# A gather, a running sum and a matmul: TensorE's program rolled into a loop, GpSimd's drain in its own stream, and another start

## The chip, the cores and the metric

The kernel runs on one core of one Trainium2 chip. Times are device microseconds of one execution. The five engines that matter here are TensorE (PE, with its weight loads shown apart as PEld), VectorE (DVE), ScalarE (ACT), GpSimd (POOL) and SyncE (SP), which only issues transfers. They run side by side and meet at counters (semaphores): an instruction raises a counter when it is done, and another waits until the counter has reached a value.

## What is computed

There are 16 batches. In each, 2048 rows of 512 numbers are picked out of 4096 by sorted indices, summed cumulatively along the 2048, and multiplied by one 512 x 512 matrix:

```python
B, S, N, D = (16, 4096, 2048, 512)
gathered = x[b_idx, indices, :].copy()
cs = np.cumsum(gathered, axis=1)
return np.matmul(cs, w).astype(np.float32)
```

So 67 MB are read by rows of 2 KB, and 67 MB are written.

## The kernel before

A *tile* is 128 gathered rows (T = 256 of them), a *group* is two tiles (G = 128). Every group passes through the same stations, and each engine has its own stream, written out in full, one instruction after the other.

- `gather(t)` on POOL (L108): one indirect transfer brings the 128 rows of tile t into `g32`. There is room for NG = 16 tiles; from the 17th on POOL waits until the tile's room is free, that is, until the cast of eight groups earlier is done (`s_c`).
- `cast(g)` on ACT (L120): both tiles of a group become 16-bit in `g16` (NH = 3 buffers), when both transfers have landed.
- `sums(t)` on PE (L128): four small matmuls with a triangular matrix `ut` put the running sums of a tile, turned on its side, into PSUM `pa` (NA = 4 buffers).
- `carry(t)` on DVE (L143, L148): adds the last column of the tile before and writes `cst` in 16 bits. This is the chain that goes through a whole batch.
- `project(g, j)` on PE (L160): four matmuls with the weights `w16` give half of a group's output in PSUM `pb` (NB = 2 buffers).
- `drain(g)` on ACT (L172): copies the group's output into `ob` (NO = 8 buffers).
- `store(g)` on SP (L178): writes it out.

The order within each engine is fixed by the program. PE's runs two groups ahead with the sums: sums of the first four tiles, then for each group g: the first sum of group g+2, the first product of g, the second sum, the second product. ACT's alternates: the cast of group g+3, then the drain of group g. So the cast of group g+4 stands behind the drain of group g, and the sums of group g+4 behind that cast.

In the beginning SP loads the indices of two tiles in a form that POOL can use directly (`idx_first`), then all indices (`idx64`), then the weights in one transfer of 1 MB. The rest of the indices is made usable on the way: DVE turns them into floats (L225), PE transposes them (L229), DVE turns them back (L234). POOL makes the constants. ACT casts group 0, then all of the weights (L252), then the next groups.

At the end SP waits for the last eight stores. The block is left by `tile_critical(no_gpsimd_drain=False)` (L78), which lets GpSimd drain after that.

Of the kernel before, what the change touches and what calls it, by code (L numbers as in the profile page):

```python
# [27 lines left out]
def kernel(  # L28
# [19 lines left out]
    FIRST = R  # L48
    NG = 16
    NH = 3  # L50
# [3 lines left out]
    NO = 8  # L54
    AH = 2
# [14 lines left out]
    ident = const.tile([P, P], FP32)  # L70
    g32 = [const.tile([P, R, D], FP32, name=f"g32_{i}") for i in range(NG // R)]
# [6 lines left out]
    ctx.enter_context(tc.tile_critical(no_gpsimd_drain=False))  # L78

    def sem(name):  # L80
        return tc.alloc_semaphore(name)

    s_first, s_w, s_ut, s_wc, s_if, s_pt, s_prep = (
        sem(f"s_{n}") for n in ("first", "w", "ut", "wc", "if", "pt", "prep")
    )
    s_idx = [sem(f"s_idx{k}") for k in range(KI)]
    s_g = [sem(f"s_g{i}") for i in range(NG)]
# [11 lines left out]
    def gather(t):  # L99
        g, r = divmod(t, R)  # L100
        pool.need(s_c, g + 1 - NG // R)
        if t < FIRST:
            pool.need(s_first, 16)
            ap = idx_first[:, t, 0:1]
        else:
            pool.need(s_prep, t // P + 1)
            ap = idxg[:, t // P, t % P : t % P + 1]
        nc.gpsimd.indirect_dma_start(  # L108
            out=g32[g % (NG // R)][:, r, :],
            out_offset=None,  # L110
            in_=x_flat,
            in_offset=bass.IndirectOffsetOnAxis(ap=ap, axis=0),
            element_offset=(t // NT) * S * D,
        ).then_inc(s_g[t % NG], 16)
# [7 lines left out]
    def sums(t):  # L122
        g, r = divmod(t, R)
        pe.need(s_c, g + 1)
        pe.need(s_ut, 4)
        pe.need(s_d, t - NA + 1)
        for c in range(DC):
            mm = nc.tensor.matmul(  # L128
                out=pa[t % NA][:, c],
                lhsT=g16[g % NH][:, r, c * P : (c + 1) * P],  # L130
                rhs=ut[:],
                start=(c == 0),
                stop=(c == DC - 1),
            )
        mm.then_inc(s_a, 1)
# [19 lines left out]
    def project(g, j):  # L155
        pe.need(s_wc, 1)
        pe.need(s_d, R * (g + 1))
        pe.need(s_e, g - NB + 1)
# [20 lines left out]


    with nc.allow_non_contiguous_dma(reason="a few indices, one per partition"):
        nc.sync.dma_start(
            out=idx_first[:],
            in_=indices[0, 0 : FIRST * P].bitcast(U32).rearrange("(t p w) -> p t w", p=P, w=2),
        ).then_inc(s_first, 16)
# [5 lines left out]
    nc.sync.dma_start(out=w32[:], in_=w.rearrange("(c p) d -> p c d", p=P)).then_inc(s_w, 16)  # L191
    for g in range(G):
        store(g)
    for g in range(G - NO, G):
        sp.need(s_o[g % NO], 16 * (g // NO + 1))

# [22 lines left out]
    for t in range(T):  # L219
        gather(t)  # L220


    for k in range(KI):
        dve.need(s_idx[k], 16)
        nc.vector.tensor_copy(out=idxf[:, k, :], in_=idx64[:, k, 0::2]).then_inc(s_if, 1)  # L225
    for k in range(KI):
# [4 lines left out]
        ).then_inc(s_pt, 1)  # L231
    for k in range(KI):
        dve.need(s_pt, k + 1)
        nc.vector.tensor_copy(out=idxg[:, k, :], in_=pb[k % NB][:, 0, :P]).then_inc(s_prep, 1)  # L234
    for t in range(T):
        carry(t)


    for t in range(R * AH):
        sums(t)  # L240
    pe.need(s_prep, KI)
    for g in range(G):
        for j in range(R):
            t = R * (g + AH) + j
            if t < T:
                sums(t)
            project(g, j)


    cast(0)  # L250
    act.need(s_w, 16)
    nc.scalar.copy(out=w16[:], in_=w32[:]).then_inc(s_wc, 1)  # L252
    for g in range(1, AH + 1):
        cast(g)
    for g in range(G):
        if g + AH + 1 < G:
            cast(g + AH + 1)
        drain(g)

# [29 lines left out]
```

## Time and profile before

| | us |
|---|---|
| four runs | 424.21, 434.3, 428.37, 464.36; median 431.34 |
| the profiled execution | 424.21 |
| its span | 422.5 |
| PE busy | 313.4 (74%) |
| PEld busy | 156.0 (37%) |
| ACT busy | 253.0 (60%) |
| POOL busy | 243.8 (58%) |
| DVE busy | 177.9 (42%) |
| moved | 135.92 MB, mean 322 GB/s |

The span is the time between the first and the last instruction of the profiled execution. A busy share is a mean over the whole span. The page also cuts the span into 40 slices of 10.56 us and gives for each the busy share of an engine in tenths (9 is 90% or more), the share of full clock that TensorE was granted, the mean busy share of the 16 DMA engines and the rate. A timeline gives the start, the length, the engine, the line, the operation with its operands, a count, and in brackets the idle time before it and what ended it; "remote" and "issue" stand where the profile shows no instruction that did. The ends of matmuls in it are modelled.

### The profile page before, as it was taken

What the parts mean: (1) busy time and instruction counts of PE and PEld (TensorE: products, weight loads), DVE (VectorE), ACT (ScalarE), POOL (GpSimd) and SP (SyncE); (2) the same over time, 40 slices, a digit from 0 to 9 for tenths busy, and PEclk for the clock granted to TensorE, in tenths of its full rate; (3) what the DMA queues carried; (4) which work ended last, traced back from release to release, by engine and by line L of the source; (5) the groups of instructions that cost most, each with busy time, mean ns of one, the idle gap of its engine ahead of it and who ended that gap; (6) DMA issues with size and microseconds to landing.
All of it is one profiled execution on the core that took longest, in us unless ns stands there. A gap on an engine that the chain in (4) does not pass through costs nothing.

```text
span 422.5 us, 5833 instructions
## 1 busy us (share of the span) xinstructions
PE 313.4 (74%) x2050; PEld 156.0 (37%) x2050; DVE 177.9 (42%) x260; ACT 253.0 (60%) x258; POOL 243.8 (58%) x264
## 2 busy tenths in 40 slices
PE   0723979775968688778787787878778787877990
PEld 0411534332534344334333343433334343333540
DVE  0302443443443445344444444444444444444640
ACT  1512655664755557566666766666676666667870
POOL 6773666555656475666666666666666666666000
PEclk9976789899899698999999999999999999999997
DMA  7775899899899899999999999999999999999752
GB/s 231 210 211 201 284 339 340 321 332 342 296 364 330 296 331 317 341 369 359 356 356 349 363 354 355 358 358 355 354 359 349 358 353 358 357 360 351 302 239 110
DMA packets 40029, 135.92 MB, mean 322 GB/s; under 512 B 6465, under 2 KB 6721, under 8 KB 40001
## 3 DMA queue, kind: packets, MB, share of 16 engines
q0 software_dynamic: 20480, 67.13, 49.1%
q1 hardware_dynamic: 19520, 68.43, 41.4%
q8 instruction: 17, 0.28, 0.3%
q14 instruction: 12, 0.09, 0.1%
HBM read 68.42 MB, written 67.11 MB: 321 GB/s over the span
## 4 chain that ended last, share of the span: by engine, by line
PE 71%; issue 16%; another core or an unknown queue 5%; ACT 3%; POOL 2%; DMA 1%; ACTq 0%; SPq 0%
PE pb L160 53%; PE pa L128 17%; ACT g L120 3%; POOL g L108 2%; DMA g<-in_x_dram,idxg 1%; DMA idx_first<-in_indices_dram 0%; ACT ob L172 0%; ACTq L23 0%; SPq L284 0%; SPq L78 0%
## 5 line engine op out<-in xcount | busy, mean ns | idle before, releaser
L108 POOL DMA_INDIRECT g<-in_x_dram,idxg x254 | 240.6, 947 | 144.3 <-issue 111.9
L160 PE MATMUL pb<-w,cst 128*128 128x512 f16 x1024 | 275.3, 394 | 0.0
L148 DVE TENSOR_TENSOR cst<-pa,cst 128x512 f16<-128x512 f32 x240 | 166.0, 692 | 209.3 <-PE pa L128 106.1
L172 ACT COPY ob<-pb 128x1024 f32<-128x1024 f32 x128 | 129.6, 1013 | 150.7 <-PE pb L160 104.3
L128 PE MATMUL pa<-ut,g 128*128 128x128 f16 x1024 | 104.8, 228 | 94.5 <-issue 62.1
L128 PEld LDWEIGHTS pa<-ut,g 128*128 128x128 f16 x1024 | 73.1, 102 | 184.8 <-issue 112.2
L120 ACT CAST g<-g 128x1024 f16<-128x1024 f32 x128 | 134.0, 1048 | 0.6 <-issue 0.6
L160 PEld LDWEIGHTS pb<-w,cst 128*128 128x128 f16 x1024 | 93.2, 101 | 66.6 <-issue 9.2
L143 DVE CAST cst<-pa 128x512 f16<-128x512 f32 x16 | 11.0, 690 | 17.1 <-PE pa L128 17.1
L120 ACT ACT_TABLE_LOAD x1 | 1.3, 1283 | 9.3 <-DMA g<-in_x_dram,idx_first 9.3
L229 PE MATMUL pb<-ident,idxf 128*128 128x128 f32 x2 | 0.7, 457 | 4.5 <-DVE idxf L225 4.5
L108 POOL DMA_INDIRECT g<-in_x_dram,idx_first x2 | 2.1, 1044 | 1.5 <-DMA idx_first<-in_indices_dram 1.2
L225 DVE CAST idxf<-idx 128x128 f32<-128x128 uint32 x2 | 0.5, 227 | 4.2 <-DMA idx<-in_indices_dram 4.1
L229 PEld LDWEIGHTS pb<-ident,idxf 128*128 128x128 f32 x2 | 0.4, 182 | 4.5 <-issue 4.5
L252 ACT CAST w<-w 128x2048 f16<-128x2048 f32 x1 | 1.9, 1893 | 0.0
L234 DVE CAST idxg<-pb 128x128 uint32<-128x128 f32 x2 | 0.6, 292 | 0.3 <-PE pb L229 0.3
L198 POOL MEMSET ident<- 128x128 f32 x1 | 0.2, 205 | 0.5 <-SPq L78 0.5
L201 POOL TENSOR_SCALAR_AFFINE_SELECT ident<-ident 128x128 f32<-128x128 f32 x1 | 0.3, 288 | 0.1
L210 POOL TENSOR_SCALAR_AFFINE_SELECT ut<-ut 128x128 f16<-128x128 f16 x1 | 0.3, 291 | 0.0
L273 POOL MEMSET const-float32-0.0<- 128x1 f32 x1 | 0.1, 100 | 0.3 <-issue 0.3
L199 POOL MEMSET ut<- 128x128 f16 x1 | 0.2, 205 | 0.0
L273 POOL MEMSET const-uint8-127<- 128x1 uint8 x1 | 0.1, 117 | 0.0
(2 smaller groups left out, 0.2 us busy)
## 6 DMA issues: line engine op xcount, KB each, us to landing
out_dram<-ob SPq DMA_DIRECT2D x128, 512.0 KB
g<-in_x_dram,idxg POOLq DMA_INDIRECT x254
w<-in_w_dram SPq DMA_DIRECT2D x1, 1024.0 KB, 5.4
idx<-in_indices_dram SPq DMA_DIRECT2D x2, 128.0 KB, 2.5
g<-in_x_dram,idx_first POOLq DMA_INDIRECT x2
idx_first<-in_indices_dram SPq DMA_DIRECT2D x1, 2.0 KB, 1.9
```

The source lines that it names most:

```text
L108: nc.gpsimd.indirect_dma_start(out=g32[g % (NG // R)][:, r, :], out_offset=None, in_=x_flat, in_offset=bass.IndirectOffsetOnAxis(ap=ap, ax ...
L120: nc.scalar.copy(out=g16[g % NH][:], in_=g32[g % (NG // R)][:]).then_inc(s_c, 1)
L128: mm = nc.tensor.matmul(out=pa[t % NA][:, c], lhsT=g16[g % NH][:, r, c * P : (c + 1) * P], rhs=ut[:], start=(c == 0), stop=(c == DC - 1),)
L143: nc.vector.tensor_copy(out=dst, in_=pa[t % NA][:]).then_inc(s_d, 1)
L148: nc.vector.tensor_tensor(out=dst, in0=pa[t % NA][:], in1=last.unsqueeze(2).broadcast_to([P, DC, R, Q]), op=mybir.AluOpType.add,).then_inc ...
L160: mm = nc.tensor.matmul(out=pb[g % NB][:, j], lhsT=cst[g % NC][:, c, j, :], rhs=w16[:, c, :], start=(c == 0), stop=(c == DC - 1),)
L172: nc.scalar.copy(out=ob[g % NO][:], in_=pb[g % NB][:]).then_inc(s_e, 1)
L201: nc.gpsimd.affine_select(out=ident[:], in_=ident[:], compare_op=mybir.AluOpType.is_equal, fill=0.0, base=0, pattern=[[-1, P]], channel_mu ...
L225: nc.vector.tensor_copy(out=idxf[:, k, :], in_=idx64[:, k, 0::2]).then_inc(s_if, 1)
L229: nc.tensor.transpose(out=pb[k % NB][:, 0, :P], in_=idxf[:, k, :], identity=ident[:]).then_inc(s_pt, 1)
L234: nc.vector.tensor_copy(out=idxg[:, k, :], in_=pb[k % NB][:, 0, :P]).then_inc(s_prep, 1)
L252: nc.scalar.copy(out=w16[:], in_=w32[:]).then_inc(s_wc, 1)
```

## The change

TensorE. A group is now worked on as: first product of g, first sum of g+2, second product, second sum (`step`). Groups 4 to 123 are a loop on the engine of 30 rounds of four groups; within it the waits compare counters with registers that are computed from the loop variable, and `sums` waits only for its cast, once a group. Before the loop, group 0 is multiplied right after its own two sums. The last three groups are written out in another order. Before and after the transposes of the indices stand nine and ten matmuls on zeros.

GpSimd. The block no longer drains it; a `drain` stands in its stream behind the last gather.

The start. Indices of four tiles instead of two are loaded directly, in two transfers, one of them from ACT's queue. The weights come in four transfers, each with its own counter; ACT casts two quarters and DVE the other two. ACT executes a copy of one element first. Group 0 is cast tile by tile.

The end. The last group is cast tile by tile, drained by DVE (first half) and ACT (second half) and stored in two transfers.

Buffers. `g16` has four instead of three.

```diff
-    FIRST = R
-    NH = 3
+    FIRST = 2 * R
+    NH = 4
+    LOOP = 4
...
-    ctx.enter_context(tc.tile_critical(no_gpsimd_drain=False))
+    ctx.enter_context(tc.tile_critical(no_gpsimd_drain=True))
...
-    def sums(t):
+    def cast_tile(t, done):
         g, r = divmod(t, R)
-        pe.need(s_c, g + 1)
-        pe.need(s_ut, 4)
-        pe.need(s_d, t - NA + 1)
+        act.need(s_g[t % NG], 16 * (t // NG + 1))
+        act.need(s_a, R * (g - NH + 1))
+        nc.scalar.copy(out=g16[g % NH][:, r], in_=g32[g % (NG // R)][:, r]).then_inc(done, 1)
+
+    def sums(t, first=0):
+        g, r = divmod(t, R)
+        if isinstance(first, int):
+            if g in (0, G - 1):
+                pe.need(s_c1 if g else s_c0, r + 1)
+            else:
+                pe.need(s_c, g)
+            pe.need(s_ut, 4)
+            pe.need(s_d, t - NA + 1)
+        elif r == 0:
+            nc.tensor.wait_ge(s_c, first + g)
...
-    def project(g, j):
-        pe.need(s_wc, 1)
-        pe.need(s_d, R * (g + 1))
-        pe.need(s_e, g - NB + 1)
+    def project(g, j, first=0):
+        if isinstance(first, int):
+            pe.need(s_wc, DC)
+            pe.need(s_d, R * (g + 1))
+            pe.need(s_e, g - NB + 1)
+        elif j == 0:
+            nc.tensor.wait_ge(s_d, R * first + R * (g + 1))
+            nc.tensor.wait_ge(s_e, first + (g - NB + 1))
...
+    def drain_last(j, lane, copy):
+        g = G - 1
+        lane.need(s_o[g % NO], 16 * (g // NO))
+        lane.need(s_b, R * g + j + 1)
+        copy(out=ob[g % NO][:, j], in_=pb[g % NB][:, j]).then_inc(s_el[j], 1)
+
+    def store_last():
+        b, h = divmod(G - 1, GB)
+        dst = out[b, h * R * P : (h + 1) * R * P, :].rearrange("(p j) d -> p j d", j=R)
+        for j in range(R):
+            sp.need(s_el[j], 1)
+            nc.sync.dma_start(out=dst[:, j], in_=ob[(G - 1) % NO][:, j]).then_inc(s_ol[j], 16)
...
-        nc.sync.dma_start(
-            out=idx_first[:],
-            in_=indices[0, 0 : FIRST * P].bitcast(U32).rearrange("(t p w) -> p t w", p=P, w=2),
-        ).then_inc(s_first, 16)
+        for k, eng in enumerate((nc.sync, nc.scalar)):
+            t = k * R
+            eng.dma_start(
+                out=idx_first[:, t : t + R, :],
+                in_=indices[0, t * P : (t + R) * P]
+                .bitcast(U32)
+                .rearrange("(t p w) -> p t w", p=P, w=2),
+            ).then_inc(s_first[k], 16)
...
-    nc.sync.dma_start(out=w32[:], in_=w.rearrange("(c p) d -> p c d", p=P)).then_inc(s_w, 16)
+    for c in range(DC):
+        nc.sync.dma_start(out=w32[:, c, :], in_=w[c * P : (c + 1) * P, :]).then_inc(s_w[c], 16)
...
     for t in range(T):
         gather(t)
+    nc.gpsimd.drain()
+
+    def busy(n):
+        pe.need(s_z, 1)
+        for _ in range(n):
+            nc.tensor.matmul(
+                out=pb[NB - 1][:, R - 1], lhsT=zeros[:, :P], rhs=zeros[:], start=True, stop=True
+            )
...
+    for c in range(DC // 2, DC):
+        dve.need(s_w[c], 16)
+        nc.vector.tensor_copy(out=w16[:, c, :], in_=w32[:, c, :]).then_inc(s_wc, 1)
     for t in range(T):
         carry(t)
-
-    for t in range(R * AH):
-        sums(t)
-    pe.need(s_prep, KI)
-    for g in range(G):
-        for j in range(R):
-            t = R * (g + AH) + j
-            if t < T:
-                sums(t)
-            project(g, j)
+    drain_last(0, dve, nc.vector.tensor_copy)
+
+    def step(g, first=0):
+        for j in range(R):
+            project(g, j, first)
+            if not isinstance(first, int) or g + AH < G:
+                sums(R * (g + AH) + j, first)
+
+    for t in range(R):
+        sums(t)
+    pe.need(s_prep, KI)
+    for j in range(R):
+        project(0, j)
+        sums(R + j)
+    for t in range(2 * R, R * (AH + 1)):
+        sums(t)
+    for g in range(1, LOOP):
+        step(g)
+    with nc.tensor.Fori(LOOP, G - LOOP, LOOP) as first:
+        for g in range(LOOP):
+            step(g, first)
+    for g in range(G - LOOP, G - AH - 1):
+        step(g)
...
-    cast(0)
-    act.need(s_w, 16)
-    nc.scalar.copy(out=w16[:], in_=w32[:]).then_inc(s_wc, 1)
+    act.need(s_z, 1)
+    nc.scalar.copy(out=spare[:], in_=zeros[:, :1])
+    for c in range(DC // 2):
+        act.need(s_w[c], 16)
+        nc.scalar.copy(out=w16[:, c, :], in_=w32[:, c, :]).then_inc(s_wc, 1)
+    for t in range(R):
+        cast_tile(t, s_c0)
     for g in range(1, AH + 1):
         cast(g)
```

## The prediction

> **What bounds the kernel now.** I read the slices first, then the table by stretches, then the timelines of the start and of the steady part, and last SP's waits for the end. The slices show three phases:
>
> ```profile
> DMA  7775899899899899999999999999999999999752
> GB/s 231 210 211 201 284 339 340 321 332 342 296 364 330 296 331 317 341 369 359 356 356 349 363 354 355 358 358 355 354 359 349 358 353 358 357 360 351 302 239 110
> ```
>
> Until about 42 us the transfers run at 200 to 230 GB/s. Until about 170 us they swing between 284 and 364. Then they lie flat near 356 up to 390, and fall off. The stretches give window and length, then busy us of PE, PEld, DVE, ACT and POOL, clock, DMA share and GB/s:
>
> ```profile
> 20.00:30.00 10.00, 2.28 (x15) 1.04 (x13) 0.69 (x1) 1.83 (x2) 7.56 (x9) 0.85 0.75 211
> 170.00:200.00 30.00, 23.22 (x161) 11.31 (x158) 13.14 (x19) 18.72 (x20) 19.08 (x21) 1.00 0.99 360
> 400.00:410.00 10.00, 10.00 (x71) 5.18 (x70) 5.53 (x8) 7.81 (x8) 0.00 (x0) 1.00 0.63 253
> ```
>
> In the steady part no engine is full, and the DMA share is 0.99. At the end only TensorE is full: the last gather is issued at 389.5, and eight groups are still to be multiplied. In the start POOL works and everybody else stands. TensorE, ACT, DVE and POOL there (start, length, what, and in brackets the idle time before it and who ended it):
>
> ```profile
> 17.95 1.91 PE L160 MATMUL pb<-w,cst 128*128 128x512 f16 x4
> 28.17 1.01 ACT L172 COPY ob<-pb 128x1024 f32<-128x1024 f32 x1 [11.21 <-remote]
> 39.50 1.01 ACT L172 COPY ob<-pb 128x1024 f32<-128x1024 f32 x1 [9.37 <-remote]
> 35.87 0.69 DVE L148 TENSOR_TENSOR cst<-pa,cst 128x512 f16<-128x512 f32 x1 [12.59 <-remote]
> 34.65 0.94 POOL L108 DMA_INDIRECT g<-in_x_dram,idxg  x1 [0.30 <-issue]
> 41.72 0.95 POOL L108 DMA_INDIRECT g<-in_x_dram,idxg  x1 [6.13 <-ACT g L120]
> ```
>
> The first drain waits only for group 0's product, whose last matmuls are shown to end at 19.86 (17.95 and 1.91), and starts at 28.17. So TensorE's results arrive 8 us late, and DVE's sum later still. They come in a burst about when POOL, after issuing gathers back to back since 3.16, has run out of free tiles. The steady part shows the same lateness, smaller:
>
> ```profile
> 241.45 1.03 PE L160 MATMUL pb<-w,cst 128*128 128x512 f16 x4
> 244.07 1.01 ACT L172 COPY ob<-pb 128x1024 f32<-128x1024 f32 x1 [1.04 <-remote]
> 244.98 1.05 ACT L120 CAST g<-g 128x1024 f16<-128x1024 f32 x1
> 246.08 0.40 PE L128 MATMUL pa<-ut,g 128*128 128x128 f16 x4 [0.64 <-issue]
> ```
>
> A group takes 2.96 us: from the 113th gather at 178.26 to the 249th at 379.38 there are 136 in 201.1, two to a group. TensorE's part is two times 1.09 (a sum and a product), with about 0.6 idle, the 0.64 above. The end:
>
> ```profile
> SPq L78 <- POOLq L78: 4.8, 1, 4.8
> ```
>
> After its last store SP stands 4.8 us for GpSimd's drain, with nothing beside it.
>
> [...] the dependents start 8.3 us (28.17) and 1.6 us (244.07 against 242.48) after the shown end. [...] The trace shows the fetching (queue q8: 17 packets, 0.28 MB, so 16 KB each) but no taken loop branch. [...]
>
> **The change part by part.** The sum is made against the profiled execution: span 422.5, time 424.2, so 1.7 around it. It is the lowest of the four times shown; their median is 431.3.
>
> *GpSimd's drain.* The drain goes from the end of the block to behind the last gather. There it begins near 391 and is over long before SP's last wait for a store ends at 416.2, even if it takes several times 4.8 us. Gain 4.8 us.
>
> *The last group.* DVE drains its first half, ACT the second, and two stores of half size follow. The final copy of 1024 columns takes 1.01; half is estimated at 0.55, so 0.45 less. The last store follows that copy at 413.56 and took 2.6 us; half of it, estimated from this and the 1.9 us of the 2 KB index load, is 2.3. I take 0.6 together, from 0 to 0.8. Its extra wait for s_ol blocks nobody.
>
> *The first tiles.* Indices for four tiles come in two loads, the second on ACT's queue, about 0.43 us of its time. The weights come in four loads: 4 times 0.43 on SP instead of one, so w's last issue is near 4 us; no store needs SP before 16 us. Tiles 2 and 3 now wait for a load instead of s_prep, but POOL's gap there was 0.31 against 0.30 elsewhere: nothing gained. ACT's table load of 1.28 us moves from 9.31 to before the data. Each half of w is cast on ACT and on DVE, about 1 us each instead of 1.89 on ACT. On ACT the casts of group 0 queue behind w's first two quarters, on DVE the first sum behind the last two; the whole w took 5.4 us, so near 8 us, and the first gather pair is awaited until 9.31 anyway. [...] TensorE then starts near 9.4 instead of 11.70, and multiplies group 0 before the sums of group 2. The first drain should come near 16 us, behind the cast of tiles 6 and 7, instead of 28.17.
>
> What is that worth? POOL limits, not ACT: up to 35.6 it issues every 1.25 us in either kernel, so the 25th gather at 33.40 cannot move. From there to the 105th at 166.67, 80 gathers take 133.3 us. In the steady part 80 take 118.3. That 15 us, with the stop of 6.13 in it, is all that a better start can return. An early drain frees tiles for POOL across most of that stop. The later swings may stay. I take half, 7.5, with 0 and 15 as ends.
>
> *Rolled loop.* 30 rounds of four groups. A round keeps its 128 loads and matmuls and gets eleven register instructions, one of which counts up, and a branch. [...] The lower end is also nothing: TensorE's fetches are 0.28 of 136 MB, under 1 us.
>
> *Order and buffers.* A product now comes before the sum beside it, and g16 has four buffers. The path from a drain by the cast (1.01 and 1.05), the first sum and the second product is one sum and one product shorter, 1.09 us per two groups. But transfers are busy at 0.99, so the next limit is there at once: nothing, up to a gain bounded below.
>
> Sum: 424.2 less 4.8, 0.6 and 7.5 gives **411**.
>
> **The rivals.** *Only the end.* POOL's burst makes the same jam later, and all of the 15 us stays lost. Then 424.2 less 5.4 is 419. For it speaks that POOL starts the same burst at 3.16; against it that drains begin 12 us earlier.
>
> *The shorter path shows.* If the 0.99 is contention and no limit, the two-group path of 5.9 us becomes 4.8, and POOL's 2.5 per group is the floor. A third of the way from 2.95 to 2.5, over 128 groups, is 19 us: 392. The flat 356 speaks against it.
>
> *The loop branch fetches, slower.* [...] Under full transfers I estimate 4 us, between the 2.5 of a small index load and the 5.4 of w. What decides is 2.4 us a round, the spare time. Beyond it, 30 times 1.6 is 48 us: 459; at 2.7 us it is 420. [...]
>
> **How the numbers follow.** Likeliest 0.53, only the end 0.20, the shorter path 0.07, the loop branch 0.20. About 2% is what a measurement of this kernel can tell from no change. The range: 396 takes in the full 15 us and a part of the shorter path; 440 takes in the loop branch at up to 3.4 us. Outside lie about 0.06 below and 0.12 above. Faster by over 2% are the likeliest and the shorter path: 0.60. Within 2% falls the end alone: 0.19. Slower: 0.21.
>
> **What would show it.** GpSimd's drain near 391 and no wait of SP for POOL at the end; the first copy of L197 near 16 us; POOL's first stop shorter than 6.13; the plateau still near 356. A gap of TensorE at each 64 sums and products would show the branch. I am wrong if the swings up to 170 us grow, or if the plateau moves.

## The result, and the profile after

The change made the kernel slower: 455.24 us median (447.91 to 460.25, 12 runs) against 444.19 us (416.39 to 464.36, 17 runs of the kernel before, the four shown among them). By medians that is 2.5%; the ratio of the fast runs, those within 1.5% of the fastest run of the same kernel, is 1.075, with a 95% interval of 1.067 to 1.083. The forecast was 411 us. The profiled execution of the changed kernel took 458.93 us, with a span of 457.2. The one of the kernel before, at 424.21, lies 20 us under its median, so the two profiles differ by more than the kernels do.

One thing has to be said before the profile, because no number below can be understood without it. The 18 experiments fell on five chips. On three of them the kernel before takes 420 to 458 us, much as in this pair, and TensorE's results reach the other engines late. On the two others it takes 356 to 359 us, and they arrive on time. I call them late chips and on-time chips. A measure of it, counted in the traces from 170 us on: DVE starts on a sum, in the median, 1.33 us after the sum's shown end in the kernel before and 1.95 us in the changed kernel on late chips, and 0.07 us in the changed kernel on an on-time chip. Each chip was used at one time only, so whether the chip or the time makes the difference can't be told. Every experiment is compared with runs of the kernel before on its own chip.

DMA share and GB/s of the changed kernel in 40 slices:

```profile
DMA  7874899888899888889888888888888888889965
GB/s 229 241 224 149 328 314 354 308 291 299 309 329 314 294 309 297 304 318 319 303 294 304 306 311 320 310 295 302 307 306 316 305 305 306 307 299 323 326 263 229
```

The flat stretch near 356 never comes. From 80 us until the last two slices the rate lies between 291 and 329. So the plateau moved, which the prediction had named as a sign of being wrong. The same stretches as before, as window and length, then busy us of PE, PEld, DVE, ACT and POOL, clock, DMA share and GB/s:

```profile
20.00:30.00 10.00, 4.45 (x16) 1.98 (x16) 1.38 (x2) 0.00 (x0) 7.56 (x9) 0.67 0.84 273
170.00:200.00 30.00, 23.40 (x145) 12.16 (x144) 11.49 (x17) 15.85 (x17) 17.17 (x19) 0.89 0.87 307
400.00:410.00 10.00, 7.00 (x44) 3.46 (x42) 3.97 (x6) 5.24 (x6) 4.75 (x6) 0.92 0.91 322
```

In the steady part PE does 145 instructions in 30 us instead of 161, POOL issues 19 instead of 21, and the DMA share has fallen from 0.99 to 0.87. No unit is full. The clock has fallen too, from 1.00 to 0.89, but TensorE is busy in 23.4 of the 30 us, as before, and idle in the rest. Late chips don't have a low clock as such: two kernels below run there at 0.997 (plain loads) and 0.99 (paced). The start (start, length, what, and in brackets the idle time before it and who ended it):

```profile
16.96 1.00 ACT L197 COPY ob<-pb 128x1024 f32<-128x1024 f32 x1
39.95 1.01 ACT L197 COPY ob<-pb 128x1024 f32<-128x1024 f32 x1 [20.48 <-remote]
34.63 0.95 POOL L117 DMA_INDIRECT g<-in_x_dram,idxg  x1 [0.30 <-issue]
42.18 0.94 POOL L117 DMA_INDIRECT g<-in_x_dram,idxg  x1 [6.60 <-ACT g L129]
```

The first drain comes at 16.96, where the forecast had put it. The second comes at 39.95, after POOL has run out of tiles at 35.6 exactly as before. POOL's stop is then 6.60 us instead of 6.13. A piece of the steady part, by engine:

```profile
186.12 1.03 PE L185 MATMUL pb<-w,cst 128*128 128x512 f16 x4
188.57 1.01 ACT L197 COPY ob<-pb 128x1024 f32<-128x1024 f32 x1 [4.49 <-PE pb L185]
190.79 0.94 POOL L117 DMA_INDIRECT g<-in_x_dram,idxg  x1 [3.97 <-ACT g L129]
195.78 1.01 ACT L197 COPY ob<-pb 128x1024 f32<-128x1024 f32 x1 [0.26 <-PE pb L185]
196.83 1.03 PE L185 MATMUL pb<-w,cst 128*128 128x512 f16 x4
199.54 0.94 POOL L117 DMA_INDIRECT g<-in_x_dram,idxg  x1 [0.30 <-issue]
202.23 1.01 ACT L197 COPY ob<-pb 128x1024 f32<-128x1024 f32 x1 [4.50 <-PE pb L185]
203.14 1.05 ACT L129 CAST g<-g 128x1024 f16<-128x1024 f32 x1
203.72 1.89 PE L185 MATMUL pb<-w,cst 128*128 128x512 f16 x4 [2.72 <-DVE cst L169]
204.46 0.94 POOL L117 DMA_INDIRECT g<-in_x_dram,idxg  x1 [3.97 <-ACT g L129]
```

This is a cycle of 13.7 us for eight gathers (190.79 to 204.46). POOL issues eight back to back, the last from 199.54, and then stops for 3.97 us. The product shown to end at 197.86 (196.83 and 1.03) is drained only at 202.23, 4.4 us later, and that is 1.7 us after POOL's last gather has ended at 200.48. Behind this drain stands the cast at 203.14, and behind the cast the gather at 204.46. So for 4 us in each 13.7 GpSimd issues nothing. The waits over the whole run (who, for whom: us in total, times, longest):

```profile
ACT ob L197 <- PE pb L185: 152.4, 78, 4.5
PE pb L185 <- ACT ob L197: 59.3, 24, 3.7
PE pb L185 <- DVE cst L169: 36.4, 23, 10.2
```

GpSimd's gathers over the whole run (busy us, mean ns, then behind the second bar the idle us before them and what ended most of it), the changed kernel first:

```profile
L117 POOL DMA_INDIRECT g<-in_x_dram,idxg x252 | 238.1, 945 | 184.1 <-ACT g L129 111.6
L108 POOL DMA_INDIRECT g<-in_x_dram,idxg x254 | 240.6, 947 | 144.3 <-issue 111.9
```

The idle time grew from 144.3 to 184.1 us; about 76 us of each are the 0.30 between gathers that follow at once. (The part put down to ACT can't be compared: in the profile before, the signals of only 33 of ACT's 128 casts are recorded.) TensorE waits at its products (pb). In the kernel before it waits at its sums (pa):

```profile
PE pa L128 <- issue: 62.1, 82, 7.9
PE pa L128 <- ACT g L120: 32.5, 9, 7.2
```

Another forecast line did come true: in SP's waits there is none for POOL any more. The 4.8 us are gone.

### The profile page after: what moved, and what is told of

It is laid out like the page before. It is cut to its first block, busy times and chain, and to the rows that moved or that the text cites. A ratio compares the mean times of both kernels' runs of the same rounds, so it can differ in the third digit from the quotient of the medians.

```text
span 457.2 us, 6060 instructions
## 1 busy us (share of the span) xinstructions
PE 346.7 (76%) x2069; PEld 178.5 (39%) x2069; DVE 178.5 (39%) x264; ACT 250.2 (55%) x262; POOL 243.2 (53%) x264
## 4 chain that ended last, share of the span: by engine, by line
PE 75%; ACT 6%; issue 6%; DVE 5%; another core or an unknown queue 5%; DMA 1%; SPq 1%; ACTq 0%; DVEq 0%
PE pb L185 61%; PE pa L149 14%; ACT ob L197 5%; DVE cst L169 4%; DMA w<-in_w_dram 1%; ACT g L129 1%; SPq L234 0%; SPq L230 0%; DVE cst L164 0%; ACT ob L209 0%; ACTq L23 0%; DVE w L294 0%; SPq L222 0%; DVEq L23 0%
## 5 line engine op out<-in xcount | busy, mean ns | idle before, releaser
L185 PE MATMUL pb<-w,cst 128*128 128x512 f16 x1024 | 308.3, 431 | 102.0 <-ACT ob L197 59.3
L117 POOL DMA_INDIRECT g<-in_x_dram,idxg x252 | 238.1, 945 | 184.1 <-ACT g L129 111.6
L185 PEld LDWEIGHTS pb<-w,cst 128*128 128x128 f16 x1024 | 96.6, 107 | 188.8 <-DVE cst L169 91.0
L129 ACT CAST g<-g 128x1024 f16<-128x1024 f32 x126 | 132.3, 1050 | 4.0 <-DMA g<-in_x_dram,idxg 2.8
L149 PEld LDWEIGHTS pa<-ut,g 128*128 128x128 f16 x1024 | 87.4, 107 | 79.6 <-issue 27.0
L149 PE MATMUL pa<-ut,g 128*128 128x128 f16 x1024 | 107.7, 233 | 2.0 <-ACT g L135 1.4
L273 PE MATMUL pb<-zeros 128*128 128x512 f16 x19 | 6.3, 498 | 1.5 <-DVE zeros L277 1.5
L117 POOL DMA_INDIRECT g<-in_x_dram,idx_first x4 | 4.0, 994 | 2.1 <-DMA idx_first<-in_indices_dram 1.2
L273 PEld LDWEIGHTS pb<-zeros 128*128 128x128 f16 x19 | 2.2, 122 | 4.4 <-issue 1.9
L135 ACT CAST g<-g 128x512 f16<-128x512 f32 x4 | 2.4, 619 | 2.2 <-DMA g<-in_x_dram,idx_first 2.2
```

What stands on the lines that cost most here:

```text
L117: nc.gpsimd.indirect_dma_start(out=g32[g % (NG // R)][:, r, :], out_offset=None, in_=x_flat, in_offset=bass.IndirectOffsetOnAxis(ap=ap, ax ...
L129: nc.scalar.copy(out=g16[g % NH][:], in_=g32[g % (NG // R)][:]).then_inc(s_c, 1)
L135: nc.scalar.copy(out=g16[g % NH][:, r], in_=g32[g % (NG // R)][:, r]).then_inc(done, 1)
L149: mm = nc.tensor.matmul(out=pa[t % NA][:, c], lhsT=g16[g % NH][:, r, c * P : (c + 1) * P], rhs=ut[:], start=(c == 0), stop=(c == DC - 1),)
L185: mm = nc.tensor.matmul(out=pb[g % NB][:, j], lhsT=cst[g % NC][:, c, j, :], rhs=w16[:, c, :], start=(c == 0), stop=(c == DC - 1),)
L273: nc.tensor.matmul(out=pb[NB - 1][:, R - 1], lhsT=zeros[:, :P], rhs=zeros[:], start=True, stop=True)
```

## The experiments

**Four runs on a late chip (kernel before 436.1 us median, 420.12 to 448.36).** The first removes the loop from the changed kernel.

```diff
-    with nc.tensor.Fori(LOOP, G - LOOP, LOOP) as first:
-        for g in range(LOOP):
-            step(g, first)
+    for g in range(LOOP, G - LOOP):
+        step(g)
```

> The changed kernel with TensorE's loop written out again: same order, buffers, start and end. Loop theory (register waits and the branch hold TensorE up, and the stall once in four groups is the loop's): the period of 13.66 us per four groups goes, 11.8 comes back, and the time falls to 410 to 425. Jam theory (TensorE's results are held back while POOL issues gathers back to back, and the new order or the fourth buffer keeps the kernel in bursts of eight gathers): no change, 448 to 460, with POOL still stopping about 4 us after every eight gathers.

Measured: 455.97 us (438.81 to 457.21; the other three from 455.03). POOL in it:

```profile
195.21 0.95 POOL L117 DMA_INDIRECT g<-in_x_dram,idxg  x1 [3.90 <-ACT g L129]
208.83 0.95 POOL L117 DMA_INDIRECT g<-in_x_dram,idxg  x1 [3.89 <-ACT g L129]
222.47 0.94 POOL L117 DMA_INDIRECT g<-in_x_dram,idxg  x1 [3.91 <-ACT g L129]
```

The cycle of 13.6 us is the same with straight code. The loop is not the cause.

The second keeps the loop and puts the sum ahead of the product again.

```diff
-        elif r == 0:
-            nc.tensor.wait_ge(s_c, first + g)
+        else:
+            if r == 0:
+                nc.tensor.wait_ge(s_c, first + g)
+            nc.tensor.wait_ge(s_d, R * first + (R * g + r - NA + 1))
...
         for j in range(R):
-            project(g, j, first)
             if not isinstance(first, int) or g + AH < G:
                 sums(R * (g + AH) + j, first)
+            project(g, j, first)
```

> The changed kernel with the order of before inside a group (the sum of g+2 ahead of the product of g), still as a loop, with the waits on the carry that this needs. Order theory (product first makes the path from a drain to the next product shorter, so ACT frees tiles in bursts): 410 to 425, POOL's gathers come in evenly spaced pairs. If order is innocent and the buffer or the loop is guilty: 448 to 460.

Measured: 436.24 us (431.38 to 440.09). By the median that is the time of the kernel before, though the fastest run of that one (420.12) isn't reached. With the old order most of the loss is gone, but nothing of the hoped gain appears.

The third leaves the order and slows GpSimd down a little.

```diff
+        pool.need(s_idle, t)
+        nc.gpsimd.memset(idle[:], 0.0).then_inc(s_idle, 1)
```

This stands behind each gather; idle has 128 columns.

> The changed kernel with a small memset on POOL after every gather, so that POOL can't issue every 1.25 us any more but about every 1.5. Jam theory: TensorE's results come through between gathers, the stops go, and a slower POOL makes the kernel faster: 405 to 430. Loop theory: no gain, 448 to 465, since POOL is slower and nothing else is changed.

Measured: 442.75 us (439.91 to 443.56). A gather came every 1.34 us instead of 1.25, because part of the 0.30 us gap between gathers took in the memset's 0.22. Bursts remained, mostly of 8 to 12, with shorter stops. The expected time was missed. With more work for GpSimd the median is 13 us under that of the kernel without its loop on the same chip, but the fastest run of the latter (438.81) is faster than all of these. So this run is a hint and settles nothing.

The fourth takes GpSimd's gathers out of the kernel before. SP loads every second row of x instead of the indexed rows, so that the bytes stay alike (135.92 MB in both profiles). The queue and the packets do not: 56412 packets instead of 40029.

```diff
-        nc.gpsimd.indirect_dma_start(
...
+        b, h = divmod(t, NT)
+        sp.need(s_c, g + 1 - NG // R)
+        rows = x[b, 2 * h * P : 2 * (h + 1) * P, :].rearrange("(p s) d -> p s d", s=2)
+        nc.sync.dma_start(
+            out=g32[g % (NG // R)][:, r, :], in_=rows[:, 0, :]
```

> The kernel of before with each gather replaced by a plain load of the same size on SP's queue (every second row; so the rows are not those of the indices and POOL issues nothing). Jam theory: TensorE's results are no longer late, no idle time of ACT or DVE ends at remote for more than 1 us, and a group takes less than 2.9 us. If the transfers themselves were the limit (356 GB/s) and lateness only their sign: still 2.9 us or more per group, about 400 to 415.

Measured: 350.79 us (350.41 to 351.06). A stretch of it (columns as above) and DVE's wait for TensorE:

```profile
150.00:250.00 100.00, 89.62 (x614) 43.85 (x612) 52.75 (x77) 74.73 (x77) 0.00 (x0) 1.00 1.04 411
DVE cst L140 <- PE pa L120: 135.7, 233, 1.6
```

The same sums, products and stores run at 411 GB/s on a chip where the kernel before takes 436.1 us. TensorE's results are on time: DVE waits for sums that are not made yet, at this line up to 1.6 us, but starts on a sum at most 0.7 us after its shown end, and ACT on a product at most 0.9. So the 356 of the profile before was not what the transfers could do. The gathers, or something that comes with them, hold the kernel.

**Four runs on an on-time chip (kernel before 357.28 us, 356.01 to 359.44).** That the kernel before takes 80 us less here was not foreseen. The first edit takes the order of the change into the kernel before.

```diff
             t = R * (g + AH) + j
+            project(g, j)
             if t < T:
                 sums(t)
-            project(g, j)
```

> The kernel before with one edit: each product is queued ahead of the sum beside it, as in the changed kernel (still three buffers for g16, the old start, the old drain at the end). Theory A, the order is the cause: ahead of every sum TensorE now waits for a drain and for DVE's sums, and each such round trip pays for results that arrive late while GpSimd issues gathers. Then this edit alone makes most of the loss: 446 to 462 us, eight gathers back to back with stops of 3 to 4 us through the whole run, GB/s near 305. Theory B, the early start is the cause (the first drain 12 us earlier locks the engines into another rhythm): 425 to 440 us, and the plateau near 356 comes back in the second half.

Measured: 355.78 us (354.97 to 356.04), ratio 0.995 (0.993 to 0.997). Neither theory's number applies on such a chip. The order gives 1.5 us here, instead of costing anything. From 170 us on GpSimd issues a gather every 1.25 us without a stop: on an on-time chip its own pace is the limit.

The second is the change without loop, order and fourth buffer; its start and end are left.

```diff
-    NH = 4
+    NH = 3
...
-            project(g, j, first)
             if not isinstance(first, int) or g + AH < G:
                 sums(R * (g + AH) + j, first)
+            project(g, j, first)
...
-    with nc.tensor.Fori(LOOP, G - LOOP, LOOP) as first:
-        for g in range(LOOP):
-            step(g, first)
+    for g in range(LOOP, G - LOOP):
+        step(g)
```

> The changed kernel without its loop, with the sum ahead of the product again and three buffers for g16: what is left of the change is its start (indices in two loads, w in four loads and on two engines, the dummy matmuls) and its end (the drain in GpSimd's own stream, the halved last group). Theory A (order): 415 to 436 us, at least 4 us under the kernel before on the same chip. Theory B (the start): 448 to 460 us, as slow as the changed kernel, with the same bursts of eight gathers.

Measured: 351.47 us (351.35 to 351.68), ratio 0.983 (0.979 to 0.987), 5.8 us less. The last gather is issued at 322.67 in it and at 322.06 in the order-only run: the start moves nothing. All of the gain lies behind that gather, 26.9 us (span 349.6) instead of 32.0 (span 354.1), where the order-only run still shows

```profile
SPq L78 <- POOLq L78: 4.8, 1, 4.8
```

The third is the paced kernel with 512 columns (PACE = 512 instead of 128).

> The changed kernel with a memset of 512 columns on GpSimd behind each gather that the next gather waits for: estimated at 0.5 us, so a gather each 1.5 to 1.7 us and never two back to back. If gathers without a gap between them hold TensorE's results back, the bursts and the stops of 3.9 us are gone, ACT's drains lag the products by less than 1 us, and the time is GpSimd's own: 256 times 1.5 to 1.7 and some 25 us at both ends, 410 to 455 us, no slower than the changed kernel although GpSimd does more. If the lateness has another cause and GpSimd is merely late, the added 0.25 to 0.45 us per gather adds up to 60 to 110 us: above 500 us.

Measured: 444.25 us (443.0 to 446.85), with a gather every 1.66 us and no stop: GpSimd's own time. The number lies in the first theory's range, but on this chip nothing is late and there was nothing to remove, so it settled nothing.

The fourth adds gathers that nobody waits for to the plainly loaded kernel.

```diff
+    for k in range(80):
+        pool.need(s_x[k % NG], 16 * (k // NG))
+        nc.gpsimd.indirect_dma_start(
+            out=side[k % NG][:],
+            out_offset=None,
+            in_=x_flat.rearrange("n (a c) -> (n a) c", c=16),
+            in_offset=bass.IndirectOffsetOnAxis(ap=idx_first[:, k % R, 0:1], axis=0),
+        ).then_inc(s_x[k % NG], 16)
+    for k in range(100):
+        pool.need(s_idle, k)
+        nc.gpsimd.memset(idle[:], 0.0).then_inc(s_idle, 1)
```

> The plainly loaded kernel of the earlier experiment (every second row instead of the indexed rows, loaded by SP), in which GpSimd has nothing to do with the data. GpSimd issues 80 gathers back to back of 128 rows of 64 bytes each into tiles that nobody reads (to about 105 us), then 100 memsets of 1024 columns, each about as long as a gather (to about 205 us), then nothing. If issuing gathers holds TensorE's results back, ACT's and DVE's waits for TensorE grow in the first stretch alone: drains in bursts or the group at 3 us and more there, against 2.6 us in the second and third. If it is the contention of the gathers' bytes, or GpSimd being busy at all, then the first stretch is like the third, or the second like the first.

Measured: 362.13 us in one run. The stretch of gathers, that of memsets, and that of neither:

```profile
20.00:100.00 80.00, 74.03 (x516) 37.05 (x514) 44.67 (x65) 62.14 (x64) 60.48 (x65) 1.00 1.01 383
110.00:200.00 90.00, 80.39 (x550) 39.27 (x548) 47.42 (x69) 67.10 (x69) 84.89 (x90) 1.00 1.04 411
215.00:300.00 85.00, 76.15 (x520) 37.01 (x517) 45.20 (x66) 63.55 (x65) 0.00 (x0) 1.00 1.04 407
```

The gathers take 6 to 7% of the rate, and TensorE works through them at the pace of the other stretches. Here they hold nobody up.

**Three runs on another late chip (kernel before 439.37 us, 425.08 to 451.53).** The changed kernel once more:

> The changed kernel as it is. In the last four runs the kernel before took 357 us and every result was seen on time; in the runs ahead of them it took 436 us and results of TensorE were seen late. Theory D, the loss of 7.5% comes only where results arrive late: if the kernel before takes near 357 us here, the changed kernel takes 349 to 352 us (its start and its end gave 5.8 us and the order alone 1.5 us there), and eight gathers in a row with stops of 3.9 us are gone; if the kernel before takes 420 to 450 us here, the changed kernel takes 448 to 460. Theory E, the change is slower whatever the lateness (the loop's waits, the order): where the kernel before takes 357 us, the changed kernel takes 375 to 385.

Measured: 460.13 us (451.25 to 466.77), as expected of a late chip. Then the kernel before with only the drain moved:

```diff
-    ctx.enter_context(tc.tile_critical(no_gpsimd_drain=False))
+    ctx.enter_context(tc.tile_critical(no_gpsimd_drain=True))
...
     for t in range(T):
         gather(t)
+    nc.gpsimd.drain()
```

> The kernel before with one edit: GpSimd's drain behind its last gather instead of at the end of the block. The step of the forecast says 4.8 us less: 352.5 us where the kernel before takes 357.3, or 4.8 under its median where it takes 420 to 450 (there within its scatter). If the drain at the end had been hidden behind the last stores anyway: no gain.

Measured: 439.21 us (421.98 to 448.32). SP's wait for POOL is gone from its list, but a gain of 4.8 us can't be seen in a scatter of 26. Inconclusive for the time. Then the whole step of order and buffers alone, which is the edit of the order above with NH = 4:

> The kernel before with the whole step Order and buffers and nothing else of the change: the product ahead of the sum and four buffers for g16. Where results come late (the kernel before at 420 to 450 us): 446 to 462 us if this step makes the loss, 420 to 445 us if the start or something else does. Where they come on time (the kernel before near 357 us): 354 to 357 us, as the order alone gave 355.8 there; a fourth buffer adds nothing.

Measured: 460.76 us (454.76 to 464.3), ratio 1.070 (1.042 to 1.097). With the old start, the old end and no loop it is as slow as the whole change.

**Four runs on a third late chip (kernel before 433.88 us, 421.61 to 457.62).** The order alone again, with three buffers:

> The order alone once more (the kernel before, product ahead of the sum, three buffers for g16), for a chip on which results come late. If the order makes the loss of the step Order and buffers: 446 to 464 us where the kernel before takes 425 to 450. If the fourth buffer makes it: 425 to 445. Where the kernel before takes 357 us it is 355.8 again.

Measured: 464.19 us (457.15 to 466.75), ratio 1.086 (1.050 to 1.123). So the loss is there without the fourth buffer. TensorE's waits in this kernel:

```profile
PE pb L160 <- ACT ob L172: 56.9, 22, 3.9
PE pb L160 <- DVE cst L148: 32.5, 20, 4.5
```

They have moved from the sums to the products, as in the changed kernel. Start and end alone:

> Start and end of the change alone once more (sum ahead of the product, three buffers, no loop). Where results come late, the steps of the forecast say 4.8 and 0.6 us for the end and 0 to 15 us for the start: 5 to 20 us under the kernel before. If the early burst makes the same jam later: within 6 us of it. Where the kernel before takes 357 us it is 351.5 again.

Measured: 435.91 us (428.15 to 450.75), ratio 1.018 (0.981 to 1.056). Neither a gain nor a loss can be told from the scatter, but the 12.9 us that the forecast gave to start and end lie outside the interval, which leaves about 8 at most. TensorE waits at its sums again, as before:

```profile
PE pa L149 <- ACT g L129: 52.1, 24, 4.2
PE pa L149 <- issue: 30.0, 21, 5.5
```

The side gathers on this chip, same kernel as above:

> Again the plainly loaded kernel with 80 gathers of 64-byte rows on GpSimd that nobody waits for, then 100 memsets of about the same length, then nothing. Where results come late in the kernel before and GpSimd's gathers are what holds them: in the first stretch (20 to 100 us) ACT and DVE wait for TensorE two to four times as long as in the other two (with gathers on a chip without lateness it was 6.7 us for ACT's drains and 31 for DVE's sums in 80 us), and GB/s falls from 383 to near 300 there; the second and third stay at 405 to 411. If the lateness comes from the gathers' bytes or from GpSimd's data being waited for, the first stretch stays at 383.

Measured: 448.31 us in one run, where the same kernel took 362.13 on the on-time chip. Its stretches, then some of TensorE's sums and products and what DVE and ACT do with them:

```profile
20.00:100.00 80.00, 11.77 (x50) 5.19 (x48) 3.36 (x5) 3.91 (x4) 60.49 (x65) 0.55 0.16 36
110.00:200.00 90.00, 79.84 (x544) 40.33 (x544) 49.10 (x71) 69.01 (x70) 84.83 (x91) 0.93 0.94 361
215.00:300.00 85.00, 75.88 (x516) 36.90 (x514) 44.90 (x65) 63.74 (x66) 0.00 (x0) 1.00 1.04 411
```

```profile
20.36 0.56 PE L124 MATMUL pa<-ut,g 128*128 128x128 f16 x4
21.85 1.03 PE L156 MATMUL pb<-w,cst 128*128 128x512 f16 x4
40.31 1.01 ACT L168 COPY ob<-pb 128x1024 f32<-128x1024 f32 x1 [23.32 <-remote]
44.86 1.91 PE L156 MATMUL pb<-w,cst 128*128 128x512 f16 x4
50.84 0.69 DVE L144 TENSOR_TENSOR cst<-pa,cst 128x512 f16<-128x512 f32 x1 [19.64 <-remote]
73.24 0.69 DVE L144 TENSOR_TENSOR cst<-pa,cst 128x512 f16<-128x512 f32 x1 [21.71 <-remote]
84.50 1.01 ACT L168 COPY ob<-pb 128x1024 f32<-128x1024 f32 x1 [42.23 <-remote]
95.76 0.69 DVE L144 TENSOR_TENSOR cst<-pa,cst 128x512 f16<-128x512 f32 x1 [21.82 <-remote]
102.11 0.95 POOL L224 DMA_INDIRECT side<-in_x_dram,idx_first  x1 [0.30 <-issue]
115.30 2.31 DVE L144 TENSOR_TENSOR cst<-pa,cst 128x512 f16<-128x512 f32 x3 [18.85 <-remote]
115.37 1.01 ACT L168 COPY ob<-pb 128x1024 f32<-128x1024 f32 x1 [28.91 <-remote]
```

This is the clearest reading of the study. Drains and products are matched by counting both in the order of the program. The drain at 84.50 is the second, that of group 1, whose product is shown to end at 22.88 (21.85 and 1.03): 62 us late. The product shown to end at 46.77 is group 2's, and it is drained at 115.37, 69 us later. The results come one at a time, in the order in which TensorE made them: group 0's product at 40.31, the sum of tile 6 (shown to end at 20.92) at 50.84, then one product that nobody waits for alone, the sum of tile 7 at 73.24, group 1's product at 84.50, the sum of tile 8 at 95.76. That is one in about 11 us, or one in nine gathers. The kernel moves 36 GB/s meanwhile, with the DMA share at 0.16. The last gather ends at 103.06; 12 us later everything that is left arrives at once, while GpSimd is busy with memsets until 204. ACT's drains wait 65.6 us of the 80 in the first stretch, against 6.7 on the on-time chip: ten times, where I had expected two to four. Bytes, a dependency and a busy GpSimd are ruled out as causes. What is left is the gathers themselves; whether it is their issuing or their packets, and whether TensorE's signals or its matmuls are late, this run doesn't tell.

The changed kernel, paced with 320 columns:

> The changed kernel with a memset of 320 columns on GpSimd behind each gather: estimated 0.38 us, a gather each 1.49 us (the run with 512 columns had one each 1.65 and took 444 us, all of it GpSimd's). Theory G, where results come late the gathers pass at a limited rate, near one in 1.48 us, and what GpSimd issues faster piles up ahead of TensorE's signals: then nothing piles up at 1.49, stops and bursts are gone, and it takes 256 times 1.49 and 21 at the ends, 402 us, 50 under the changed kernel. Theory H, GpSimd's own waits were the brake and the late signals only follow: 455 or more. Where the kernel before takes 357 us it is 402 under either.

Measured: 417.79 us (417.59 to 418.42), ratio to the kernel before 0.986 (0.976 to 0.997), and 37 to 42 us less than the changed kernel took on late chips. The longest wait of ACT's drains is 1.8 us instead of 4.5:

```profile
ACT ob L202 <- PE pb L190: 130.6, 101, 1.8
```

GpSimd is slower at every gather, and the kernel is faster than the changed one. The results are no earlier for it: from 170 us on DVE starts on a sum 2.95 us after its shown end in the median, and at most 4.42. But they hardly make GpSimd stop any more: four short stops are left. The expected 402 was not reached: the last gather is issued at 389.88 and 26.8 us follow, where the estimate had 21 for both ends.

**Three runs on a second on-time chip (kernel before 356.75 us, 355.82 to 357.13).** Start and end with the sum first, paced by 320 columns and by 256 (edits as above):

> The start and end of the change with the sum ahead of the product (three buffers, no loop), and a memset of 320 columns on GpSimd behind each gather. With a gather each 1.50 us nothing piles up ahead of TensorE's signals where they come late, whatever the order: 256 times 1.50 and 21 to 25 us, 405 to 412 us, at least 15 under the kernel before, no stop of GpSimd over 2 us. If the remaining lateness of some 1.6 us costs as much in this order as in the other: 418 as with the product first. Where the kernel before takes 357 us: 400 to 408, slower.

> The same with 256 columns, estimated at a gather each 1.44 us. If the gathers pass at one in 1.48 us where results come late, this piles up slowly: stops come back, at 420 to 436 us. If they pass at 1.44: 256 times 1.44 and 25, 390 to 396 us. Where the kernel before takes 357 us: 388 to 394.

Measured: 403.88 us (403.47 to 404.35) with a gather every 1.50 us, and 390.73 (390.57 to 391.45) with one every 1.44. Both are GpSimd's own time, 1.133 and 1.097 times the kernel before. What order and pace do together on a late chip was not measured. Pacing is no improvement in itself: it costs 10 to 13% where results come on time. The changed kernel beside them:

> The changed kernel on the same chip as the two paced ones. Where the kernel before takes 420 to 450 us: 448 to 462. Where it takes near 357: 349 to 352 if the loss comes only with late results, 375 to 385 if the change costs 7% in itself.

Measured: 351.26 us (351.12 to 351.34), ratio 0.985 (0.983 to 0.987). So the changed kernel is 1.5% faster where results come on time. Where they don't, it was slower both times, by 2.5 and 4.7% in the medians. Its rate, steady part, and first two drains there:

```profile
GB/s 216 226 301 355 392 403 383 415 415 415 417 415 416 415 416 412 415 414 416 416 417 416 413 407 410 410 415 414 416 411 412 407 414 414 413 413 415 392 203 240
170.00:200.00 30.00, 26.76 (x185) 13.03 (x182) 15.90 (x23) 22.20 (x23) 22.69 (x25) 1.00 1.03 415
```

```profile
16.89 1.00 ACT L197 COPY ob<-pb 128x1024 f32<-128x1024 f32 x1
19.39 1.00 ACT L197 COPY ob<-pb 128x1024 f32<-128x1024 f32 x1
```

The second drain comes 2.5 us after the first one, not 23 us.

GpSimd's rhythm says it all together. I count gathers from 170 us on; a stop is an interval over 2 us between the starts of two gathers:

| kernel | chip | us per gather | stops | mean stop | gathers between stops |
|---|---|---|---|---|---|
| before | late | 1.48 | 1 | 2.4 | - |
| changed | late | 1.71 | 19 | 4.7 | 8 |
| changed, no loop | late | 1.71 | 19 | 4.8 | 8 |
| before, order and buffers | late | 1.71 | 19 | 4.8 | 8 |
| before, order alone | late | 1.71 | 19 | 4.8 | 8 |
| changed, sum first | late | 1.57 | 27 | 3.0 | 2 to 8 |
| start and end alone | late | 1.59 | 28 | 2.8 | 2 to 14 |
| before, drain moved | late | 1.65 | 25 | 3.4 | 2 to 8 |
| changed, paced by 320 | late | 1.52 | 4 | 2.2 | 34 |
| changed | on-time | 1.25 | 0 | - | - |

The profiled execution of the kernel before is one of its faster ones and hardly stops. With only the drain moved, an execution of 444.94 us has 25 stops. So bursts and stops come with the old order too, in part of the executions, and that may be where the scatter comes from. With the product in front and no pacing, every profile on a late chip has 19 or 20 stops of 4.5 to 4.8 us, nearly all with eight gathers between them.

## Why the prediction was wrong

**The step that failed is Order and buffers, "transfers are busy at 0.99, so the next limit is there at once: nothing".** Measured alone on late chips, it costs 21 us in the median with four buffers (460.76 against 439.37, ratio 1.070) and 30 us with three (464.19 against 433.88, ratio 1.086). The order is the cause; the fourth buffer isn't needed for it. The step saw a path that gets 1.09 us shorter; on an on-time chip it is worth 1.5 us in all. It didn't ask what is queued behind the product while the product waits. A product waits for a drain of two groups earlier and for DVE's sums, and both are answers to signals of TensorE itself. Where these come late, the drains come late, the casts stand behind the drains on ACT, and GpSimd waits for the casts: the timeline of the changed kernel shows this chain at 202.23, 203.14 and 204.46. Why it costs more with the product in front is argued, not shown. By the program, a product that waits for DVE now holds up the first sum of two groups on, which went ahead of it before. The wait lists show only that TensorE's waits move from the sums to the products. That it locks at eight gathers fits the timeline, where ACT makes four casts (eight tiles) between two long waits, but was only argued too.

**The reading under it failed too.** A DMA share of 0.99 at 356 GB/s was taken for the limit. That was my estimate, and no run had shown it. The plainly loaded kernel moves 411 GB/s on a late chip at share 1.04, and the changed kernel 415 on an on-time one at 1.03. The plateau was one gather in 1.48 us, GpSimd's pace under late results: a gather reads 262 KB, and as much is written for it, which makes 354 GB/s at 1.48 us and 419 at the 1.25 of an on-time chip. So a DMA share of 0.99 didn't mean that no more bytes could pass.

**The first tiles.** The drain at 16 us was right (16.96), and that an early drain "frees tiles for POOL across most of that stop" was wrong: the next one is at 39.95 and the stop is 6.60 instead of shorter. The 7.5 us were not there, neither on a late chip (435.91 against 433.88) nor on on-time ones, where GpSimd never stops and the last gather is issued 0.4 to 0.6 us later than with the old start (order-only kernel). The rival *Only the end* had this half right: "POOL's burst makes the same jam later".

**GpSimd's drain and the last group** were right: 5.4 us in the sum, 5.1 measured behind the last gather (26.9 instead of 32.0), and 5.8 with start and end alone and 5.5 with the whole change on on-time chips.

**The base** has a share in the miss. The sum starts at 424.2, the lowest of the four times shown; the median of 17 runs is 444.19. Of the 44 us between 411 and 455.24, 20 lie there. And the profile of that run, with its flat plateau and one stop, hid how the kernel runs at other times.

**The rolled loop** costs nothing that can be seen. The sum had nothing for it either, by an estimate of mine. On one late chip the changed kernel takes 460.13 us and the kernel before with order and buffers, without a loop, 460.76. The instruction queue of the changed kernel (packets, MB, share):

```profile
q8 instruction: 1, 0.02, 0.0%
```

One packet in the whole run, where the kernel before has 17: with 30 rounds, the branch back did not bring a fetch each time. So the wait for 4 us a round that the slower rival supposed did not occur. It was my estimate, and no trace had shown one. The trace records the compare-and-branch at 208 ns in the median of 30, one register instruction of each round at 44, and 270 of the 300 others at 32. A round's branch, the one of 44 and ten of 32 are 0.57 us together, where the forecast took 2.4 us as spare. None of it can be seen in the time.

**The slower rival was the wrong one.** The loop's branch was priced, the queue order was not. Yet the lines were there: a drain at 28.17 for a product shown to end at 19.86, and results that came when POOL had stopped. I read the lateness as a matter of the start and did not carry it into the step on the order, though the steady part showed 1.6 us of it.

**What stays open.** Why GpSimd's gathers delay TensorE's results, and what makes one chip do it and another not, no run shows. For every run on record there is a span from the profiler, and in profiles of late chips with gathers many records of signals are missing (33 of ACT's 128 casts are there in the kernel before, and 24 waits of TensorE's weight loads are put down to a cast; with plain loads it is 126 waits, and in the changed kernel on an on-time chip 120). Whether the recording has a part in the delay was not tested. The version to keep is start and end alone: 351.47 us on an on-time chip, as good as the whole change, and on a late one no loss is shown, though the interval of 0.981 to 1.056 leaves room for one.

## What to carry to other kernels

When a consumer starts long after its producer is shown to end (here 1.33 to 1.95 us in the median), treat that lateness as a price on every round trip of the engine, and ask of each reordering what stands behind the instruction that waits for an answer to its own signal. A DMA share of 0.99 at 360 GB/s was no limit here: with plain loads 411 passed. So before a share is taken for one, replace the suspect by a plain transfer and see whether the rate rises. Compare kernels beside each other on the same chip, and where two runs of the same kernel differ by 20% (here 357 and 436 us), find out what differs before explaining anything else.

## What was not expected of the hardware

- On three of five chips TensorE's results came late while GpSimd issued indirect DMAs (by 1.33 us in the median in the kernel before, 1.95 in the changed one). With 80 gathers that nobody waits for (share 0.16) they came by up to 69 us late, one result in about 11 us; during memsets of about the same length (1.01 us each, a gather 0.95) they came all at once after 12 us. On an on-time chip ACT's drains waited 6.7 of 80 us in the same kernel, instead of 65.6.
- On the late chips GpSimd still stopped with a gather each 1.25 us (stops of 4.7 us on average in the changed kernel) and each 1.34 us. At 1.50 the results were still 2.95 us late, but GpSimd hardly stopped.
- One core alone moved 411 to 417 GB/s, read and written together.
